# One matmul per level for both token tiles of a recurrence, its keys mixed by ScalarE

## The chip, the cores and the metric

The kernel runs on one core of a Trainium2 chip. A core has five engines that run side by side, each through its own list of instructions in order: TensorE (PE in the profile; PEld is its weight load), VectorE (DVE), ScalarE (ACT), GpSimd (POOL) and SyncE (SP), which issues most DMAs. The metric is the device time of one execution in microseconds. Three runs of the kernel before took 2759.31, 2762.63 and 2767.03 us (median 2762.63). Less is better.

## The reference

One layer over 2048 tokens of width 1024, in float32: a mixer, then a feed-forward block with a causal convolution. The mixer has two groups of four heads each, differential attention and a gated recurrence (HGRN2):

```python
proj = h @ w_in[l]                      # dq, dk, dv | hq, hf, hi, hg
# attention: a query sees all keys whose chunk of 64 tokens is not later than its own
mask = k_chunk[None, :] <= q_chunk[:, None]
a = softmax(q0 k0) - lam * softmax(q1 k1);  o = a @ v
# recurrence, chunks of 64 tokens: f = lb + (1 - lb) * sigmoid(f_logit), k = 1 - f
b = cumsum(log f)                       # within the chunk
att[t, s] = sum_k q[t, k] k[s, k] exp(b[t, k] - b[s, k])   for s <= t
o = att @ v + (q * exp(b)) @ state
state = exp(b_last) * state + (k * exp(b_last - b))^T @ v
x = x + concat([o_diff, o_hgrn]) @ w_out;   x = x + ConvGLU(RMSNorm(x))
```

The order of tokens inside a pair of 64-token chunks is free as long as the causal order of the recurrence and the mask of the attention follow it: attention sums over keys, and each output row goes back to its own token.

## The kernel before

The mixer stage goes over four sections `s`, one per head pair (one attention head, one recurrence head), and inside a section over eight blocks of 256 tokens, `BLK`; a block is two token tiles of 128 (`g` or `j` is 0 or 1). For each block it runs projections (`proj_a`, `proj_b`, `proj_c`, matmuls in fp32r with tiles `WA`, `WB`, `WC`), transposes, attention (`attn`, `attn_o`) and the recurrence (`hgrn`, `hgrn_o`). Sections and blocks are interleaved: the projections of block b+1 run beside the attention and the recurrence of block b. The step order is a string (`ORDER`, `O0`, `OF`), and on top of it the instructions of a block are merged by the program's scheduler, so that the matmuls of several steps alternate on TensorE.

The recurrence works without divisions. `hgrn` builds the decay products by doubling: `LEVELS` are half widths h of 1, 2, 4, ... 64. At level h a token tile of 128 is cut into groups of 2h; queries of the later half of each group meet keys of the earlier half. Three tiles are updated in place: `qP` holds queries times decay, `kS` keys times decay, `TT` the products of whole groups. One level does this:

- two matmuls (L441), one per token tile: the stationary operand is `kS` of the tile (127 to 64 columns), the moving operand the 64 queries of the later halves; the result is `lt[:, g]`, in PSUM. These are plain float32, and the profile shows each as two records.
- two predicated copies on DVE (L444), one per token tile: what the byte mask `lmask` marks is put into the attention tile `att[g]` of 128 x 128.
- three products on DVE (L449, L450, L452): the queries of the later halves times the first half's product, the keys of the earlier halves times the second half's, and the new `TT`.

The next level's matmuls read the new `qP` and `kS`; `lt` has one PSUM buffer (`HB=1`, shared with `op` and `sp` of `hgrn_o`), so they also wait for both copies. `hgrn_o` then multiplies `att` with the values and updates the state. The attention tiles rotate over three buffers. The scores `sc` of the attention also have one buffer: matmuls fill it, DVE takes the maximum (L367), ACT the exponential (L378), and only then may the next scores be written.

`load_rest` makes the masks once, on POOL, during the first block. The stage after the mixer, `load_o`, reads the mixer's output back, transposes it on TensorE and splits it by ACT and DVE (L555, L556) for the output projection. The later stages (up projection, down projection) are not touched.

Of the kernel before, what the change touches and what calls it, by code (L numbers as in the profile page):

```python
# [25 lines left out]
TOP, FEW, SMALL, SMALL2 = 480, 192, 320, 192  # L26
# [34 lines left out]

@with_exitstack
def hymba_kernel(ctx, tc, x, ln1_w, w_in, q_norm_w, k_norm_w, lam_q1, lam_k1, lam_q2, lam_k2,
                 diff_subln_w, hgrn_lb_logits, hgrn_norm_w, w_out, ln2_w, w_up, conv_w, conv_b,
                 w_down, out):
# [52 lines left out]
    lmask = few.tile([P, 7, 64], U8, name="lmask")  # L118
    NATT = 3
    atts = [cst.tile([P, P], F32, name=f"att{n}") for n in range(NATT)]  # L120
# [14 lines left out]
    def load_rest(tmp, tmq):  # L135
        lamv = tmp[:, 0:256].rearrange("p (n e) -> p n e", n=4)
        lbd = tmp[:, 256:268].rearrange("p (n e) -> p n e", n=3)
        lmf = tmq[:, 0:448].rearrange("p (l e) -> p l e", l=7)
# [27 lines left out]
        for li, h in enumerate(LEVELS):  # L166
            v = lmf[:, li, :].rearrange("p (n h) -> p n h", h=h)
            n = 64 // h
            for pat, base, mul in (([-2 * h, n], 0, 1), ([2 * h, n], h - 1, -1)):
                POOL.affine_select(out=v, in_=v, pattern=[pat, [0, h]], compare_op=ALU.is_ge,  # L170
                                   fill=0.0, base=base, channel_multiplier=mul)
        POOL.tensor_copy(out=lmask, in_=lmf)
        for a in atts:
            POOL.memset(a, 0.0)
# [10 lines left out]
    with ExitStack() as ms:  # L185
        wp = pool(ms, "wp", 1)
        kv = pool(ms, "kv", KVB, side="right")
# [25 lines left out]
        def phase1(b):  # L213
# [3 lines left out]
            for j in range(2):  # L217
                xt = pb.tile([P, D], F32, name="xt", tag="p")
                dma(out=xt, in_=x[b * BLK + j * P:b * BLK + (j + 1) * P, :])
                xts.append(xt)  # L220
# [35 lines left out]
        for s in range(4):  # L256
# [87 lines left out]
            def attn(b, j):  # L344
# [9 lines left out]
                for si, (k0, k1) in enumerate(segs):  # L354
                    for c in range(2):
# [8 lines left out]
                        if last:  # L364
                            DVE.memset(sc[0:64, w - 64:w], -3.0e38)
# [61 lines left out]
            def hgrn(b):  # L427
# [481 lines left out]
```

## Time and profile before

| | us |
|---|---|
| median of three runs | 2762.63 |
| the profiled execution | 2761.66 |
| its span in the trace | 2760.0 |
| TensorE busy (share of the span) | 2662.2 (96%) |
| VectorE busy | 1892.9 (69%) |
| ScalarE busy | 1212.4 (44%) |
| GpSimd busy | 1053.6 (38%) |

The mixer stage lasts from the start to about 1230 us of the span; the output projection follows until about 1600, the up projection until about 2100, the down projection to the end. Busy time is the union of an engine's records, and the end of a matmul's record is modelled: consecutive matmuls overlap in the trace. What a matmul takes on a full TensorE is therefore read from start to start.

### The profile page before, as it was taken

To read this page: it belongs to the slowest core of one execution; us is meant where nothing else is said; L and a number is where in the kernel's file an instruction comes from. 1 tells how busy PE (TensorE), PEld (TensorE's weight loads), DVE (VectorE), ACT (ScalarE), POOL (GpSimd) and SP (SyncE) were. 2 spreads that over 40 slices of the span, in tenths; PEclk is the share of its full clock that TensorE was granted. 3 is DMA by queue.
4 is the path that set the end of the run, shared out by engine and by line. 5 is a ranking of instruction groups with operands and counts; after the bars stand their busy time and mean duration, and the time that the engine had idled before them with its cause. 6 is when DMAs were issued, how large, how long until landed. Compare 5 with 4: busy or idle time off the path is not lost. (4 is left out here: it accounts for less than half of the span.)

```text
span 2760.0 us, 43193 instructions
## 1 busy us (share of the span) xinstructions
PE 2662.2 (96%) x15170; PEld 2329.6 (84%) x15170; DVE 1892.9 (69%) x4051; ACT 1212.4 (44%) x2878; POOL 1053.6 (38%) x1153
## 2 busy tenths in 40 slices
PE   7999999999999999989999999999999998899999
PEld 6888999999999999978877888887888886687887
DVE  4667855676667666773338666668777768978787
ACT  4555544454345444454335344345434434334332
POOL 2222222212222222220334443444344347877775
PEclk9999999999999999999999999999999999999999
DMA  5333422232222322125754232225222234775754
GB/s 183 119 109 112 130 89 86 82 124 83 99 83 75 115 91 84 50 88 172 248 192 142 83 92 75 86 92 175 77 85 91 70 92 129 170 159 132 178 172 168
DMA packets 273494, 322.96 MB, mean 117 GB/s; under 512 B 19470, under 2 KB 238974, under 8 KB 269182
## 3 DMA queue, kind: packets, MB, share of 16 engines
q1 hardware_dynamic: 266366, 295.04, 32.8%
q0 software_dynamic: 6912, 25.17, 5.3%
q8 instruction: 120, 1.97, 0.3%
q14 instruction: 96, 0.79, 0.1%
HBM read 198.50 MB, written 104.86 MB: 110 GB/s over the span
## 5 line engine op out<-in xcount | busy, mean ns | idle before, releaser
L684 PE MATMUL q<-xT,WS 128*128 128x512 f32 x704 | 274.4, 390 | 2.4 <-DVE xT L617 2.4
L683 PE MATMUL q<-xT,WS 128*128 128x512 f32 x704 | 274.4, 390 | 0.5 <-ACT xT L616 0.5
L685 PE MATMUL q<-xT,WS 128*128 128x512 f32 x704 | 274.3, 390 | 0.6 <-DVE WS L617 0.4
L797 PE MATMUL pd<-TW,SG 128*128 128x512 f32 x616 | 245.1, 399 | 21.2 <-DVE acc L803 7.1
L799 PE MATMUL pd<-TW,SG 128*128 128x512 f32 x616 | 243.2, 396 | 2.2 <-DVE SG L617 2.2
L798 PE MATMUL pd<-TW,SG 128*128 128x512 f32 x616 | 244.0, 397 | 0.5 <-DVE TW L617 0.5
L616 ACT CAST WS<-st 128x512 fp32r<-128x512 f32 x176 | 108.4, 618 | 243.6 <-PE q L685 227.1
L684 PE MATMUL q<-xB,WS 128*128 128x512 f32 x528 | 205.9, 390 | 2.2 <-DVE xB L617 2.2
L685 PE MATMUL q<-xB,WS 128*128 128x512 f32 x528 | 206.1, 390 | 1.2 <-DVE WS L617 1.2
L683 PE MATMUL q<-xB,WS 128*128 128x512 f32 x528 | 205.8, 390 | 0.7 <-ACT xB L616 0.7
L378 ACT ACTIVATE p<-sc,nm 128x1024 f32<-128x1024 f32 (+4 forms) x192 | 165.7, 863 | 90.3 <-DVE nm L367 87.5
L617 POOL TENSOR_TENSOR WS<-st,WS 128x512 fp32r<-128x512 f32 x44 | 88.2, 2004 | 278.4 <-ACT WS L616 258.8
L252 PE MATMUL pj<-WA,hT 128*128 128x384 f32 x512 | 176.4, 344 | 4.1 <-DVE hT L239 4.1
L367 DVE TENSOR_REDUCE nm<-sc 128x1 f32<-128x1024 f32 (+4 forms) x192 | 174.5, 909 | 6.9 <-PE sc L363 4.3
L253 PE MATMUL pj<-WA,hT 128*128 128x384 f32 x512 | 175.3, 342 | 0.0
L254 PE MATMUL pj<-WA,hT 128*128 128x384 f32 x512 | 174.5, 341 | 0.0
L797 PEld LDWEIGHTS pd<-TW,SG 128*128 128x128 f32 x616 | 118.1, 192 | 52.1 <-DVE acc L803 7.6
L684 PEld LDWEIGHTS q<-xT,WS 128*128 128x128 f32 x704 | 132.3, 188 | 30.4 <-DVE xT L617 3.1
L685 PEld LDWEIGHTS q<-xT,WS 128*128 128x128 f32 x704 | 132.3, 188 | 29.0 <-DVE WS L617 1.4
L683 PEld LDWEIGHTS q<-xT,WS 128*128 128x128 f32 x704 | 132.4, 188 | 28.6 <-ACT xT L616 0.9
L616 ACT CAST WS<-rawu 128x512 fp32r<-128x512 f32 x132 | 82.0, 623 | 159.2 <-PE q L685 159.2
L252 PE MATMUL pjc<-hT,WC 128*128 128x256 f32 x512 | 151.6, 296 | 0.2 <-ACT ig L321 0.2
(412 smaller groups left out, 7857.3 us busy)
## 6 DMA issues: line engine op xcount, KB each, us to landing
hT<-hTd SPq DMA_DIRECT2D x24, 2048.0 KB, 7.9
rawu<-in_w_up_dram SPq DMA_DIRECT2D x176, 256.0 KB, 3.1
x2d<-acc POOLq DMA_DIRECT2D x48, 512.0 KB, 6.5
gd<-c SPq DMA_DIRECT2D x176, 128.0 KB, 1.8
G<-gd SPq DMA_DIRECT2D x24, 768.0 KB, 4.2
xt<-in_x_dram SPq DMA_DIRECT2D x32, 512.0 KB, 4.1
hTd<-hT SPq DMA_DIRECT2D x8, 2048.0 KB, 6.2
qT<-qh SPq DMA_DIRECT2D x256, 64.0 KB, 2.0
```

What stands on the lines that cost most here:

```text
L252: PE.matmul(dst, lhsT=lh, rhs=rh, start=dt == 0, stop=False)
L253: PE.matmul(dst, lhsT=lh, rhs=rl, start=False, stop=False)
L254: PE.matmul(dst, lhsT=ll, rhs=rh, start=False, stop=dt == ND - 1)
L367: DVE.tensor_reduce(out=nm, in_=sc[:, 0:w], axis=AX.X, op=ALU.max, negate=True)
L378: ACT.activation(out=p[:, 0:w], in_=sc[:, 0:w], func=AF.Exp, bias=nm, accum_out=l)
L616: ACT.copy(dst[:, 0], src)
L683: PE.matmul(dst, lhsT=w[:, 0, cs], rhs=b_[:, 0, dt], start=dt == 0, stop=False)
L684: PE.matmul(dst, lhsT=w[:, 0, cs], rhs=b_[:, 1, dt], start=False, stop=False)
L685: PE.matmul(dst, lhsT=w[:, 1, cs], rhs=b_[:, 0, dt], start=False, stop=dt == 3)
L797: PE.matmul(pd, lhsT=Sx[n][:, 0, k], rhs=w[:, 0], start=k == 0, stop=False)
L798: PE.matmul(pd, lhsT=Sx[n][:, 0, k], rhs=w[:, 1], start=False, stop=False)
L799: PE.matmul(pd, lhsT=Sx[n][:, 1, k], rhs=w[:, 0], start=False, stop=k == len(qs) - 1)
```

## The change

1. In the mixer the second token tile of each block now runs backwards: the host hands over a second copy of `x`, `xm`, whose odd tiles of 128 rows are reversed, and `phase1` reads that one. The mask of the attention follows (`attn`), and `load_o` turns the odd tiles round again while it reads the transposed tile from PSUM (`tv[:, :, ::-1]`).
2. With the mirrored tile the earlier halves of tile 0 and the earlier halves of tile 1 stand in complementary columns. At each level ACT copies these 64 + 64 keys into a new tile `kp` of 128 columns (two buffers), and one matmul with 128 stationary and 128 moving columns replaces the two of 64. Its result has both tiles' products in `lt`, and the predicated copies, now over all 128 partitions, take what their mask marks. In the last block of the last section DVE makes the copy.
3. The masks are two sets (28 selects on POOL, 14 before), the attention tiles four (two per token tile), and both lie in a pool of their own at the top of the memory during the mixer. A padding is 64 bytes smaller.

```diff
-TOP, FEW, SMALL, SMALL2 = 480, 192, 320, 192
+TOP, FEW, SMALL, SMALL2 = 480, 128, 320, 192
+def view(a, off, *dims):
+
+    return bass.AP(a.tensor, a.offset + off, [list(a.ap[0])] + [list(d) for d in dims if d[1] > 1])
...
-                dma(out=xt, in_=x[b * BLK + j * P:b * BLK + (j + 1) * P, :])
+                dma(out=xt, in_=xm[2 * b + j])
...
                         if last:
-                            DVE.memset(sc[0:64, w - 64:w], -3.0e38)
+                            if j:
+                                DVE.memset(sc[64:P, w - P:w - 64], -3.0e38)
+                            else:
+                                DVE.memset(sc[0:64, w - 64:w], -3.0e38)
...
-        POOL.tensor_copy(out=lmask, in_=lmf)
-        for a in atts:
+        POOL.tensor_copy(out=lmask[:, :, 0:7], in_=lmf)
+        for a in atts[0] + atts[1]:
             POOL.memset(a, 0.0)
...
+        mc = pool(ms, "mc", 1, side="right")
+        lmask = mc.tile([P, 2, 8, 64], U8, name="lmask")
+        atts = [[mc.tile([P, P], F32, name=f"att{g}{n}") for n in range(2)] for g in range(2)]
...
-                att = [atts[(2 * b + g) % NATT] for g in range(2)]
+                att = [atts[g][b % 2] for g in range(2)]
                 for li, h in enumerate(LEVELS):
-                    nb = BLK // (2 * h)
-                    nk = P - h
+                    n, m = 64 // h, P // h
+                    qv = view(qP, h, (P - h, 2), (2 * h, n), (1, h))
+                    kl = view(kS, 0, (2 * h, n), (P + h, 2), (1, h))
+                    kf = view(kS, 0, (P + h, 2), (2 * h, n), (1, h))
                     lt = ps.tile([P, 2, 64], F32, name="lt", tag=HT, bufs=HB)
-                    qv = qP.rearrange("p (n two h) -> p n two h", two=2, h=h)
-                    kvw = kS.rearrange("p (n two h) -> p n two h", two=2, h=h)
-                    for g in range(2):
-                        ng = nb // 2
-                        PE.matmul(lt[0:nk, g].rearrange("p (n h) -> p n h", h=h), lhsT=kS[:, g * P:g * P + nk],
-                                  rhs=qv[:, g * ng:(g + 1) * ng, 1, :], start=True, stop=True)
+                    kp = wk.tile([P, P], F32, name="kp", tag="kp", bufs=2)
+                    kd = view(kp, 0, (2 * h, n), (h, 2), (1, h))
+                    if s == 3 and b == NB - 1:
+                        DVE.tensor_copy(out=kd, in_=kl)
+                    else:
+                        ACT.copy(kd, kl)
+                    PE.matmul(view(lt, 0, (64, 2), (h, n), (1, h)), lhsT=kp, rhs=qv, start=True, stop=True)
                     for g in range(2):
                         DVE.copy_predicated(
-                            out=att[g][0:nk].rearrange("p (n two h) -> p n two h", two=2, h=h)[:, :, 1, :],
-                            mask=lmask[0:nk, li].rearrange("p (n h) -> p n h", h=h),
-                            data=lt[0:nk, g].rearrange("p (n h) -> p n h", h=h))
+                            out=att[g].rearrange("p (n two h) -> p n two h", two=2, h=h)[:, :, 1 - g, :],
+                            mask=lmask[:, g, li].rearrange("p (n h) -> p n h", h=h),
+                            data=lt[:, g].rearrange("p (n h) -> p n h", h=h))
...
-                cs = slice(hf * 512, hf * 512 + 512)
-                ACT.copy(oT[0][:, cs], tp)
-                DVE.tensor_tensor(out=oT[1][:, cs], in0=tp, in1=oT[0][:, cs].bitcast(F32), op=ALU.subtract)
+                tv, (oh, ol) = tp.rearrange("p (q c) -> p q c", c=P), [
+                    t[:, hf * 512:hf * 512 + 512].rearrange("p (q c) -> p q c", c=P) for t in oT]
+                if i % 2:
+                    tv = tv[:, :, ::-1]
+                ACT.copy(oh, tv)
+                DVE.tensor_tensor(out=ol, in0=tv, in1=oh.bitcast(F32), op=ALU.subtract)
```

The three products of a level stay three instructions of the same size, written with `qv`, `kf` and `T` by the new views. The loop that makes the masks runs over both `g`.

How this stands on the engines is shown at the turn from section 1 to section 2 (the recurrence of the last block of a section beside the first projections of the next one). TensorE, from the first level to the second, before:

```order
L441 MATMUL lt<-qP,kS 127x64 x2
L252 MATMUL pj<-WA,hT 128x384
L253 MATMUL pj<-WA,hT 128x384
L254 MATMUL pj<-WA,hT 128x384
L252 MATMUL pj<-WA,hT 128x384
L362 MATMUL sc<-kst,qT 128x512
L363 MATMUL sc<-kst,qT 128x512
L362 MATMUL sc<-kst,qT 128x384
L363 MATMUL sc<-kst,qT 128x384
L441 MATMUL lt<-qP,kS 126x64 x2
```

And with the change:

```order
L454 MATMUL lt<-qP,kp 128x128
L259 MATMUL pj<-WA,hT 128x384
L260 MATMUL pj<-WA,hT 128x384
L258 MATMUL pj<-WA,hT 128x384
L259 MATMUL pj<-WA,hT 128x384
L368 MATMUL sc<-kst,qT 128x512
L369 MATMUL sc<-kst,qT 128x512
L368 MATMUL sc<-kst,qT 128x384
L369 MATMUL sc<-kst,qT 128x384
L454 MATMUL lt<-qP,kp 128x128
```

The same eight matmuls stand between two levels; the two level matmuls have become one.

VectorE at the fifth level of the same block, before (the copies, the product of the queries, that of the keys, with attention's small operations between):

```order
L444 COPY_PREDICATED att_92<-lmask,lt 112x4x16
L444 COPY_PREDICATED att_90<-lmask,lt 112x4x16
L449 TENSOR_TENSOR qP<-qP,TT 128x8x16
L382 SCALAR_TENSOR_TENSOR l_8370<-l,wv 128x1
L450 TENSOR_TENSOR kS<-kS,TT 128x8x16
```

With the change:

```order
L456 COPY_PREDICATED att_186<-lmask,lt 128x4x16
L456 COPY_PREDICATED att_188<-lmask,lt 128x4x16
L460 TENSOR_TENSOR qP<-qP,TT 128x2x4x16
L391 SCALAR_TENSOR_TENSOR l_8494<-l,wv 128x1
L461 TENSOR_TENSOR kS<-kS,TT 128x2x64
```

The product of the keys now stands two levels ahead of that of the queries: its tile has the shape of the seventh level beside the fifth level's copies.

ScalarE around the first levels of the same block, before (`p,l<-sc` is the exponential of the scores, `qr`, `vst` and `qn` belong to the next block's projections):

```order
L485 ACTIVATE op,ssh<-o_8304 128x128
L378 ACTIVATE p,l<-sc,nm 128x1024
L283 COPY qr<-pj 128x256
L284 COPY vst<-pj 128x128
L286 ACTIVATE qn<-qr 128x256
L372 ACTIVATE wv<-nm,nm_8346 128x1
L378 ACTIVATE p,l<-sc,nm_8346 128x896
L283 COPY qr<-pj 128x256
```

With the change:

```order
L496 ACTIVATE op,ssh<-o_8428 128x128
L387 ACTIVATE p,l<-sc,nm 128x1024
L453 COPY kp<-kS 128x128
L289 COPY qr<-pj 128x256
L290 COPY vst<-pj 128x128
L292 ACTIVATE qn<-qr 128x256
L453 COPY kp<-kS 128x128
L381 ACTIVATE wv<-nm,nm_8470 128x1
L387 ACTIVATE p,l<-sc,nm_8470 128x896
L453 COPY kp<-kS 128x128 x2
L289 COPY qr<-pj 128x256
```

Nothing has changed places; the copies into `kp` are put in between. Those of levels one and two stand further up, before the last exponentials of the block before.

## Rows read from the trace of the kernel before

**Rows 1.** Stretches of the mixer: length, busy PE PEld DVE ACT POOL, PE clock

```profile
60.00:300.00 240.00, 227.87 (x1672) 214.24 (x1670) 170.00 (x550) 131.01 (x376) 64.14 (x126) 1.00 0.33 113
300.00:620.00 320.00, 313.71 (x2316) 296.41 (x2316) 217.18 (x731) 153.20 (x449) 70.33 (x135) 1.00 0.31 99
620.00:920.00 300.00, 294.58 (x2164) 279.48 (x2165) 202.36 (x686) 140.55 (x418) 69.29 (x133) 1.00 0.29 95
920.00:1230.00 310.00, 296.15 (x2143) 277.86 (x2142) 207.62 (x686) 141.78 (x414) 73.62 (x129) 0.98 0.24 79
```

**Rows 2.** The tile lt: what TensorE waited for before its matmuls (us, times)

```profile
  DVE kS L450: 13.3, 18
```

**Rows 3.** Timeline of TensorE, first level of one block: start, duration (us), instruction

```profile
621.26 0.34 PE L254 MATMUL pj<-WA,hT 128*128 128x384 f32 x1
621.43 0.56 PE L441 MATMUL lt<-qP,kS 128*127 128x64 f32 x4
621.80 0.42 PE L252 MATMUL pj<-WA,hT 128*128 128x384 f32 x1
622.05 0.34 PE L253 MATMUL pj<-WA,hT 128*128 128x384 f32 x1
```

**Rows 4.** Timeline of TensorE, seventh and last level of the same block

```profile
635.59 0.28 PE L254 MATMUL pj<-WB,hT 128*128 128x256 f32 x1
635.71 0.28 PE L252 MATMUL pj<-WB,hT 128*128 128x256 f32 x1
635.92 0.45 PE L441 MATMUL lt<-qP,kS 128*64 128x64 f32 x4
636.30 0.38 PE L253 MATMUL pj<-WB,hT 128*128 128x256 f32 x1
636.52 0.28 PE L254 MATMUL pj<-WB,hT 128*128 128x256 f32 x1
```

**Rows 5.** Timeline of TensorE, a lone float32 matmul of 128 by 128

```profile
868.11 0.33 PE L253 MATMUL pj<-WA,hT 128*128 128x384 f32 x1
868.28 0.39 PE L477 MATMUL sp<-ig,kt__11715 128*128 128x128 f32 x2
868.42 0.42 PE L254 MATMUL pj<-WA,hT 128*128 128x384 f32 x1
868.68 0.34 PE L252 MATMUL pj<-WA,hT 128*128 128x384 f32 x1
868.86 0.33 PE L253 MATMUL pj<-WA,hT 128*128 128x384 f32 x1
```

**Rows 6.** ScalarE on a 128x128 tile, memory to memory: min/median/max ns

```profile
L323 ACT ACTIVATE sg<-ig x64: 296/310/334, 35.5 to 1179.1; 128x128 f32<-128x128 f32 x64
```

**Rows 7.** Predicated copies, two levels, 60 to 1230 us: busy us, mean ns

```profile
L444 DVE COPY_PREDICATED att<-lmask,lt 126x64 f32<-126x64 uint8 x62 | 15.7, 304 | 3.3 <-PE lt L441 2.1
L444 DVE COPY_PREDICATED att<-lmask,lt 120x64 f32<-120x64 uint8 x64 | 12.2, 222 | 4.3 <-PE lt L441 4.3
```

**Rows 8.** Timeline of VectorE, fifth level of the block of Rows 3

```profile
630.97 0.36 DVE L444 COPY_PREDICATED att<-lmask,lt 112x64 f32<-112x64 uint8 x2 [0.38 <-PE lt L441]
631.24 0.28 DVE L449 TENSOR_TENSOR qP<-qP,TT 128x128 f32<-128x128 f32 x1
631.57 0.29 DVE L450 TENSOR_TENSOR kS<-kS,TT 128x128 f32<-128x128 f32 x1
```

**Rows 9.** The tile sc: what its engines waited for (us, times)

```profile
  ACT p L378: 21.8, 54
```

**Rows 10.** Timeline of GpSimd, the masks

```profile
18.58 6.03 POOL L170 TENSOR_SCALAR_AFFINE_SELECT tmq<-tmq 128x64 f32<-128x64 f32 x14
...
28.42 0.19 POOL L98 TENSOR_SCALAR rq_m<-ssq 128x4 f32<-128x4 f32 x1 [3.19 <-DVE ssq L288]
```

**Rows 11.** Groups by line, 1200 to 1600 us: the split in load_o

```profile
L556 DVE TENSOR_TENSOR oT<-tpo,oT 128x512 fp32r<-128x512 f32 x32 | 21.8, 686 | 7.4 <-ACT oT L555 7.4
L555 ACT CAST oT<-tpo 128x512 fp32r<-128x512 f32 x32 | 18.3, 582 | 52.9 <-PE tpo L553 52.9
```

More of the change, by code (lines that the diff above doesn't have):

```diff
@@ L64, in hymba_kernel @@
                  diff_subln_w, hgrn_lb_logits, hgrn_norm_w, w_out, ln2_w, w_up, conv_w, conv_b,
-                 w_down, out):
+                 w_down, xm, out):
     nc = tc.nc
@@ L117, in hymba_kernel @@
     hgw = cst.tile([P, P], F32, name="hgw")
-    lmask = few.tile([P, 7, 64], U8, name="lmask")
-    NATT = 3
-    atts = [cst.tile([P, P], F32, name=f"att{n}") for n in range(NATT)]
     def load_ln1(tp):
@@ L137, in load_rest @@
         lbd = tmp[:, 256:268].rearrange("p (n e) -> p n e", n=3)
-        lmf = tmq[:, 0:448].rearrange("p (l e) -> p l e", l=7)
+        lmf = tmq[:, 0:896].rearrange("p (g l e) -> p g l e", g=2, l=7)
         for hf in range(2):
@@ L165, in load_rest @@
         POOL.memset(lmf, 1.0)
[L166 to L171, printed above, removed]
-        POOL.tensor_copy(out=lmask, in_=lmf)
-        for a in atts:
+        for g in range(2):
+            for li, h in enumerate(LEVELS):
+                v = lmf[:, g, li, :].rearrange("p (n h) -> p n h", h=h)
+                n = 64 // h
+                for pat, base, mul in (([-2 * h, n], -g * h, 1), ([2 * h, n], h - 1 + g * h, -1)):
+                    POOL.affine_select(out=v, in_=v, pattern=[pat, [0, h]], compare_op=ALU.is_ge,
+                                       fill=0.0, base=base, channel_multiplier=mul)
+        POOL.tensor_copy(out=lmask[:, :, 0:7], in_=lmf)
+        for a in atts[0] + atts[1]:
             POOL.memset(a, 0.0)
@@ L446, in hgrn @@
-                            mask=lmask[0:nk, li].rearrange("p (n h) -> p n h", h=h),
-                            data=lt[0:nk, g].rearrange("p (n h) -> p n h", h=h))
-                    Tv = T.rearrange("p (n two) -> p n two", two=2)
-                    DVE.tensor_tensor(out=qv[:, :, 1, :], in0=qv[:, :, 1, :], in1=Tv[:, :, 0:1].broadcast_to([P, nb, h]), op=ALU.mult)
-                    DVE.tensor_tensor(out=kvw[:, :, 0, :], in0=kvw[:, :, 0, :], in1=Tv[:, :, 1:2].broadcast_to([P, nb, h]), op=ALU.mult)
@@ L451, in hgrn @@
-                    Tn = TT[:, to:to + nb]
-                    DVE.tensor_tensor(out=Tn, in0=Tv[:, :, 0], in1=Tv[:, :, 1], op=ALU.mult)
+                            out=att[g].rearrange("p (n two h) -> p n two h", two=2, h=h)[:, :, 1 - g, :],
+                            mask=lmask[:, g, li].rearrange("p (n h) -> p n h", h=h),
+                            data=lt[:, g].rearrange("p (n h) -> p n h", h=h))
+                    DVE.tensor_tensor(out=qv, in0=qv, in1=view(T, 0, (m + 1, 2), (2, n), (0, h)), op=ALU.mult)
@@ L453, in hgrn @@
+                    DVE.tensor_tensor(out=kf, in0=kf, in1=view(T, 1, (m - 1, 2), (2, n), (0, h)), op=ALU.mult)
+                    Tn = TT[:, to:to + m]
+                    DVE.tensor_tensor(out=Tn, in0=view(T, 0, (2, m)), in1=view(T, 1, (2, m)), op=ALU.mult)
                     T = Tn
-                    to += nb
+                    to += m
                 HG[b] = (qk, kS, qP, T)
@@ L458, in hgrn_o @@
                 qk, kS, qP, T = HG.pop(b)
-                att = [atts[(2 * b + g) % NATT] for g in range(2)]
+                att = [atts[g][b % 2] for g in range(2)]
                 for g in range(2):
@@ L903 @@
         args.append(nc.dram_tensor(f"in_{name}_dram", a.shape, mybir.dt.from_np(a.dtype), kind="ExternalInput").ap())
+    xm = np.array(inputs["x"]).reshape(S // P, P, D)
+    xm[1::2] = xm[1::2, ::-1]
+    arrays["in_xm_dram"] = xm
+    args.append(nc.dram_tensor("in_xm_dram", xm.shape, F32, kind="ExternalInput").ap())
     args.append(nc.dram_tensor("out_0_dram", (1, S, D), F32, kind="ExternalOutput").ap())
```

## The prediction, before the result was known

> **What bounds the kernel now.** I read the engines' busy time by stretches first, then the waits at the tile that the change touches, then the timeline of TensorE at that place. In the mixer, where all of the edit but one detail lies, TensorE is busy 227.87 + 313.71 + 294.58 + 296.15 = 1132.3 of 1170 us between 60 and 1230 us, at a granted clock of 0.98 to 1.00, its level of 2.4 GHz; VectorE is busy some two thirds of that time and ScalarE under half (153.20 of 320 us in the second stretch) [rows 1]. The reader is to see there that only 38 us are free on TensorE. So this stage ends when TensorE has worked off its list, and what counts is how long each group of matmuls holds it, and what it newly waits for. The recurrence looks like a chain (matmul, copies, products, next matmul), but its links are hidden between other matmuls: TensorE stood before the level matmuls 18 times, 13.3 us in all, over 224 levels [rows 2].
>
> **The change part by part.** *Level matmuls.* There are 4 sections x 8 blocks x 7 levels = 224 levels. What a group costs is read from start to start. At the first level the matmul before it starts at 621.26 and the second one behind it at 622.05: 0.79 us, in which two 384-column matmuls stand that take 0.175 each in an undisturbed stream (868.68 to 868.86 is 0.18); so the four records of the group cost 0.79 - 0.35 = 0.44 us [rows 3, 5]. At the seventh level it is 636.52 - 635.71 = 0.81, less two of 256 columns at 0.12: 0.57 [rows 4]. Seven groups of this block read this way; the first and last are shown, and the five between give 0.44, 0.44, 0.42, 0.40 and 0.36. The mean is 3.07 / 7 = 0.439 us, so the level matmuls hold TensorE for 224 x 0.439 = 98 us.
>
> With the change a level is one float32 matmul of 128 by 128, two records. That shape is in the trace: between two 384-column matmuls it costs 868.68 - 868.11 - 0.35 = 0.22 us [rows 5]. I take this value. The step from its own start to the next one is 0.14, so it can't cost less than that (saving 67 us), and from above it is bounded by the 0.44 of the four records (saving nothing). The saving is 224 x (0.439 - 0.22) = 49 us, and nothing lies beside it: the engine is full, and the same matmuls stand between two levels as before, in the same order.
>
> The row shows that a group's time goes with its count of records, about 0.11 us each, and little with the columns that move (64 or 128) [rows 3, 5]. The Trainium skill (TensorE: Matmul & The Clock Gate, Back-to-back issue gap) gives for an isolated stream about 60 cycles up to 64 columns and 134 at 128: four short ones then cost 240 cycles and two long ones 268, the change would save nothing, and the sum would stand at some 2764 us by that estimate. The same page (LDWEIGHTS) has a weight load at its columns / 1.2 ns, 107 ns for 128: two loads fewer would save 213 ns a level, 48 us, also an estimate. The trace agrees with the second.
>
> *The copies into kp.* 217 on ScalarE and 7 on VectorE (the last block). The nearest row, a 128 x 128 operation of ScalarE from memory to memory, takes 310 ns [rows 6]: 217 x 0.31 = 67 us. It is spread over the mixer, some 17 us on a section of about 300 us where ScalarE works 153 of 320 [rows 1]; it becomes 55% busy. The first two levels' copies pick single keys or pairs in turn from two tiles. A fine pattern has a price on VectorE here: the predicated copy takes 304 ns at the second level and 222 at the fourth [rows 7]. With the same 0.08 us on 62 of the copies ScalarE has 5 us more, which its idle time hides as well.
>
> What may come onto the path is the copy's place: the level matmul now waits for ScalarE. What takes the edge off is that the product of the keys no longer waits for a level matmul, only for the copy; it is issued two levels ahead. From the copies' start at 630.97 the queries' product is done at 631.52 and the keys' at 631.86 [rows 8]; the later one leaves the path between two levels, 0.34 us, and a matmul with half the records gives its result sooner. Behind a copy that waits on ScalarE stand the next block's `qr`, `vst`, `qn` and the exponentials of the scores, and TensorE waits for those, the exponential before all, as `sc` has one buffer: 21.8 us in 54 waits now, weight loads included [rows 9].
>
> The trace doesn't show the new wait, so I bound it: from below the present 13.3 us at the level matmuls could vanish (-13 us) [rows 2]; from above every copy stands in the chain with its full 0.31 us (+67 us) [rows 6]. Between ends so far apart I take the value nearest to a row: half of the 13.3 us once more, +7 us, because ScalarE's free time and the lead of two levels speak for little.
>
> *VectorE.* Two predicated copies and three products a level as before, of the same count of elements; 7 copies more. Nothing. If four-dimensional patterns cost 0.08 us as above on six operations of a level or so, VectorE would have some 224 x 0.4 = 90 us more and at 75% to 80% would still not bound.
>
> *Masks.* 14 more selects, 6 us, stand on GpSimd ahead of `rq_m`, which waited 3.19 us for its input before; it slips by some 3 us [rows 10]. The projections that TensorE has in hand then cover it; without that cover it would cost those 3 us once.
>
> *The reversed read in `load_o`.* 16 of the 32 operations of each engine, 582 and 686 ns [rows 11]. If each took twice as long, 16 x (0.58 + 0.69) = 20 us on engines that are not full in that stage; I cost it at nothing. `xm` is read as `x` was. The tiles' new places cost nothing that a row could show.
>
> **Sum.** Against the profiled execution of 2761.7 us (the median of the runs is 1 us more): 2761.7 - 49 + 7 = 2720 us, 1.5% faster.
>
> **The rivals.** *The saving comes back in part as waits at the new link.* For it: ScalarE's list is worked off in order, and some copies stand right behind an exponential of about 1 us or ahead of two levels' matmuls. Against it: the order puts them early. If half the copies' time shows, 33 us in place of 7: 2761.7 - 49 + 33 = 2746 us.
>
> *Time goes with the columns that move.* Then nothing is saved and the copies hide: 2762 us and up to 7 more. (The first of the two rules of the Trainium skill above, TensorE: Matmul & The Clock Gate, would have it so.) Against it stand the four records at 0.44 us beside the two at 0.22 [rows 3, 5]; for it only that the lone matmul shown is followed by fp32r work, so that part of its load could be covered. No change.
>
> *ScalarE's list blocks the attention (the other side).* A copy waits for TensorE's level matmul two levels back, since `kp` has two buffers; the exponential of the scores stands behind it, and the next scores on TensorE wait for that. There are 192 exponentials; if each comes 0.35 us later (a copy with its wait) and the one score buffer passes all of it on, that is 67 us: 2761.7 - 49 + 67 = 2780 us. It decides from 49 / 192 = 0.26 us for each exponential. For it: 54 such waits exist already [rows 9]. Against: ScalarE is free half of the time, so a delay of one is made up before the next.
>
> **How the numbers follow.** My forecast (2700 to 2735) has 0.68, the partial return (2735 to 2753) 0.16, the columns or an almost full return 0.08, the blocked attention 0.08. What a measurement can tell from no change is 0.3%, about 8 us: below 2754 is faster. So faster 0.84, same 0.08, slower 0.08. The range goes from the saving with the present waits gone (2761.7 - 49 - 13 = 2700) up into the partial return, 2750.
>
> **What would show it.** Right: two records per level, 448 in all, their group at 0.22 to 0.28 us between fp32r matmuls; the mixer shorter by 40 to 50 us and the later stages as long as before; ScalarE 60 to 75 us busier; waits of TensorE at the level matmuls below 25 us. Wrong: the level group at 0.4 us (the price of the matmul failed), idle time of TensorE in the mixer well above 38 us with ScalarE named as releaser of `lt` or `sc` (the place of the copy failed), or the stage after the mixer longer by several us (the reversed reads).

## The result, and the profile after

The changed kernel takes 2786.5 us (median; 2783.2 to 2787.0) against 2762.6 for the kernel before beside it: a ratio of 1.0083 with a 95% interval of 1.0071 to 1.0096. It is slower by 0.8%, where 1.5% faster was forecast. Its profiled execution took 2783.2 us, with a span of 2781.4; before it was 2761.7 and 2760.0, so 21.4 us are to be found.

First the stretches of the mixer, with the columns of [rows 1] (busy PE, PEld, DVE, ACT, POOL, then the clock):

```profile
60.00:300.00 240.00, 222.68 (x1559) 208.28 (x1558) 162.79 (x538) 137.37 (x411) 61.62 (x123) 0.98 0.30 108
300.00:620.00 320.00, 308.21 (x2213) 288.46 (x2212) 222.12 (x738) 170.56 (x513) 69.63 (x137) 1.00 0.31 101
620.00:920.00 300.00, 292.39 (x2072) 273.85 (x2072) 205.94 (x697) 155.94 (x483) 69.48 (x135) 1.00 0.30 96
920.00:1230.00 310.00, 289.91 (x2025) 268.69 (x2024) 211.04 (x692) 155.91 (x471) 73.15 (x130) 0.97 0.23 72
```

TensorE is still busy 1113 of 1170 us, with fewer instructions. ScalarE has 17 us more in the second stretch, as forecast for one of this length, and 53 us more in the four together, where 60 to 75 were named. So the mixer has not become idle, and it has not become much shorter either. Where the time went is read from the first and last starts of three tiles: `pjc`, the mixer's last projection; `ot`, the load of the first output rows for the output projection; `q` from `xT`, the up projection (it starts at 1450 us, and not at about 1600, as the section on the time before has it). The numbers are x count, ns (min/median/max), first and last start. Before the change:

```profile
L254 PE MATMUL pjc<-hT,WC x512: 274/283/386, 39.3 to 1192.3; 128*128 128x256 f32 x171
L545 SPq DMA_DIRECT2D ot<-od x16: 319/382/431, 1189.7 to 1406.6; - x16
L683 PE MATMUL q<-xT,WS x704: 387/389/628, 1450.4 to 2293.3; 128*128 128x512 f32 x176
```

After it:

```profile
L260 PE MATMUL pjc<-hT,WC x512: 277/283/365, 39.8 to 1186.2; 128*128 128x256 f32 x171
L556 SPq DMA_DIRECT2D ot<-od x16: 320/376/423, 1248.1 to 1425.8; - x16
L697 PE MATMUL q<-xT,WS x704: 387/389/793, 1468.9 to 2315.2; 128*128 128x512 f32 x176
```

The mixer's last projection ends 6.1 us earlier (1192.3 to 1186.2). From there to the up projection it took 258.1 us, now 282.7: 24.6 us more. The rest of the program takes 2.9 us more (1309.6, 1312.5). -6.1 + 24.6 + 2.9 = 21.4. So there are two questions: why the handover from the mixer to the output projection lost 24.6 us, and why the mixer won 6 and not 42.

The handover first. `ot` was loaded at 1189.7, when the last block's recurrence had not yet begun, and its projection (`pjo`) filled TensorE between the last levels. Before the change:

```profile
1217.11 0.93 PE L441 MATMUL lt<-qP,kS 128*124 128x64 f32 x4
1217.80 0.77 PE L599 MATMUL pjo<-wo,oT 128*128 128x512 f32 x1
...
1220.69 0.39 PE L599 MATMUL pjo<-wo,oT 128*128 128x512 f32 x1
1220.92 0.53 PE L441 MATMUL lt<-qP,kS 128*120 128x64 f32 x4
```

Now `ot` is loaded at 1248.1. The timeline of the changed kernel there (start, duration, instruction, idle time before it and what ended it):

```profile
1208.56 0.77 PE L454 MATMUL lt<-qP,kp 128*128 128x128 f32 x2 [3.72 <-DVE kp L451]
...
1213.70 0.77 PE L454 MATMUL lt<-qP,kp 128*128 128x128 f32 x2 [1.94 <-DVE kp L451]
...
1247.73 0.32 SPq L434 DMA_DIRECT2D od<-oo  x1
1248.10 0.42 SPq L556 DMA_DIRECT2D ot<-od  x1
...
1251.78 1.97 PE L564 MATMUL tpo<-ident,ot 128*128 128x128 f32 x8 [6.12 <-DMA ot<-od]
...
1254.89 0.63 PE L614 MATMUL pjo<-wo,oT 128*128 128x512 f32 x1
1255.32 0.63 PE L615 MATMUL pjo<-wo,oT 128*128 128x512 f32 x1
```

In SyncE's list the load now stands right behind the mixer's last write (1247.73, 1248.10). TensorE has only some score matmuls to put between the last levels and waits there for a copy three times (3.72, 1.94 and 1.77 us). The first projection matmuls follow each other at 0.43 us (1254.89 to 1255.32), against 0.23 at 1340 us. The clock granted from 1250 to 1256 us is 0.50, the level of 1.2 GHz, after a wait of 6.12 us for the load. By thirds of a stretch of 90 us, before:

```profile
1190.00:1220.00 30.00, 20.69 (x125) 17.83 (x124) 24.19 (x51) 16.95 (x36) 12.34 (x10) 0.83 0.57 184
1220.00:1250.00 30.00, 28.34 (x188) 24.62 (x187) 20.87 (x51) 13.32 (x33) 3.43 (x8) 1.00 0.09 29
1250.00:1280.00 30.00, 29.76 (x155) 24.92 (x154) 8.55 (x16) 10.81 (x29) 2.73 (x7) 1.00 0.48 158
```

and after:

```profile
1190.00:1220.00 30.00, 15.99 (x67) 11.92 (x67) 27.94 (x67) 14.67 (x29) 10.48 (x10) 0.72 0.38 112
1220.00:1250.00 30.00, 20.12 (x125) 17.67 (x123) 12.29 (x34) 10.31 (x28) 4.87 (x8) 0.79 0.06 16
1250.00:1280.00 30.00, 27.32 (x119) 22.33 (x120) 5.50 (x8) 5.46 (x14) 0.74 (x2) 0.86 0.39 134
```

468 matmuls became 311 (14 of the difference are records saved at the levels), and the granted clock fell from 1.00 to 0.79 in the middle third.

Why the load went there is not in the trace; it follows from the memory map of the two programs (bytes per partition). The change puts 3,072 bytes at the top and two copies of `kp`, 1,024 bytes, into the working pool, so all pools of that side lie 4,096 bytes lower; the pools of the other side lie 2,048 lower. The output projection's last tile, `ht`, lay at 132,096 to 136,192 before, over the mixer's projection pool, which is done early. Now it lies at 130,048 to 134,144 and covers 704 bytes of `sm` (133,440 to 136,164), the small statistics, which are in use until the mixer's last output. If the scheduler therefore holds the projection's first steps back until the statistics are free, a shift of the pools alone must bring the loss and take it away; that is tested below.

### The profile page after: what moved, and what is told of

It reads as the page before. It is cut to its first block, busy times and chain, and to the rows that moved or that the text cites. A ratio compares the mean times of both kernels' runs of the same rounds, so it can differ in the third digit from the quotient of the medians.

```text
span 2781.4 us, 42701 instructions
## 1 busy us (share of the span) xinstructions
PE 2650.1 (95%) x14722; PEld 2305.0 (83%) x14722; DVE 1900.0 (68%) x4058; ACT 1263.6 (45%) x3095; POOL 1051.6 (38%) x1168
## 5 line engine op out<-in xcount | busy, mean ns | idle before, releaser
L425 PE MATMUL av<-vst,aT 128*128 128x128 f32 x1088 | 153.0, 283 | 7.6 <-ACT aT L422 7.2
```

## The experiments

All times are medians; a ratio is to the kernel before, run on the same chip (2762.4 to 2763.7 us). Two theories stood first. "Places": the tiles' new places cost the handover, whatever the recurrence does. "ScalarE in the key path": the copies of the mixed keys block the attention and the last block. Each predicts a slower kernel, by about as much.

### The places

The recurrence of before at the new places:

```diff
-TOP, FEW, SMALL, SMALL2 = 480, 192, 320, 192
+TOP, FEW, SMALL, SMALL2 = 480, 128, 320, 192
...
-    lmask = few.tile([P, 7, 64], U8, name="lmask")
...
-    atts = [cst.tile([P, P], F32, name=f"att{n}") for n in range(NATT)]
...
+        mc = pool(ms, "mc", 1, side="right")
+        mcs = mc.tile([P, 2, 8, 64], U8, name="lmask")
+        lmask = mcs[:, 0, 0:7]
+        atts = [mc.tile([P, P], F32, name=f"att{n}") for n in range(NATT)]
+        mc.tile([P, P], F32, name="attpad")
...
+        wk.tile([P, 2 * P], F32, name="kpad", tag="kpad", bufs=1)
```

> The recurrence of the kernel before, untouched, with the change's places alone: mask and attention tiles at the top, 1,024 bytes more in the working pool, so that the output projection's pools lie where they lie in the changed kernel. Theory 'places': the projection's first load of the outputs again stands behind all of the mixer's writes, the stretch from the last block's diagonal to the up stage grows by some 20 to 26 us (248 to 270-274), and the whole comes to 2780-2789 us. Theory 'ScalarE in the key path': nothing of the recurrence has changed, so 2762 us within 0.3%.

Measured 2786.5 us, ratio 1.0087 (1.0073 to 1.0101): the whole loss, with not one instruction of the recurrence changed.

```profile
L258 PE MATMUL pjc<-hT,WC x512: 274/283/386, 38.5 to 1191.3; 128*128 128x256 f32 x171
L549 SPq DMA_DIRECT2D ot<-od x16: 319/380/424, 1255.1 to 1432.0; - x16
L687 PE MATMUL q<-xT,WS x704: 388/389/628, 1476.1 to 2317.7; 128*128 128x512 f32 x176
```

The mixer ends as before (1191.3), `ot` comes at 1255.1, and the handover takes 284.8 us. The reverse, the changed recurrence with the old places:

```diff
+    lmask = few.tile([P, 2, 8, 64], U8, name="lmask")
+    atts = [[cst.tile([P, P], F32, name=f"att{g}{n}") for n in range(1)] for g in range(2)]
...
-        mc = pool(ms, "mc", 1, side="right")
-        lmask = mc.tile([P, 2, 8, 64], U8, name="lmask")
-        atts = [[mc.tile([P, P], F32, name=f"att{g}{n}") for n in range(2)] for g in range(2)]
...
-                att = [atts[g][b % 2] for g in range(2)]
+                att = [atts[g][0] for g in range(2)]
```

> The changed recurrence with mask and attention tiles back at their old place (one attention tile per token tile instead of two, so that they fit). Theory 'places': the handover is as before the change (248 us from the last block's diagonal to the up stage), what the mixer gained stays, 2752-2760 us. Theory 'ScalarE in the key path': the loss stays, 2780-2787 us.

Measured 2756.1 us, ratio 0.9978 (0.9968 to 0.9987).

```profile
L259 PE MATMUL pjc<-hT,WC x512: 274/283/365, 39.5 to 1181.6; 128*128 128x256 f32 x171
L555 SPq DMA_DIRECT2D ot<-od x16: 319/379/431, 1179.2 to 1397.4; - x16
L696 PE MATMUL q<-xT,WS x704: 388/389/796, 1440.5 to 2286.1; 128*128 128x512 f32 x176
```

The handover takes 258.9 us again. Third, the changed kernel with its tiles at the top but one attention tile per token tile (`for n in range(1)` in place of `range(2)`), so that the pools rise by 1,024 bytes and `ht` ends where `sm` does not yet begin (134,144 and 134,464):

> The changed kernel with one attention tile per token tile instead of two, still at the top; this alone moves the pools on that side up by 1,024 bytes, and the projection's last tile no longer lies over the statistics of the mixer. Theory 'places': as good as with the old places, 2752-2760 us, the same within 0.2%. Theory 'ScalarE in the key path': 2780-2787 us. A third, that it matters which bank or end of the memory the masks lie at, would set it apart from the kernel with the old places.

Measured 2757.8 us, ratio 0.9981 (0.9973 to 0.9990). With that the top of the memory is cleared: 1,024 bytes decide on 29 us, and "places" holds. "ScalarE in the key path" falls as the cause of the loss. That it is the overlap of `ht` and `sm`, and no other of the shifted tiles, follows from the map; no run moved `ht` alone.

### What the merge is worth

That leaves the mixer. Without the mixed tile, at the old places (`lhsT=kp` becomes `lhsT=kS[:, 0:P]`, and the copies go; it leaves tile 1's keys out):

> As the changed recurrence at the old places, but without the mixed tile: the shared matmul reads tile 0's keys for both token tiles, which leaves tile 1's keys out of the diagonal. It prices the mixing. Theory 'ScalarE in the key path': without 224 copies and the wait at each level the mixer gives back what the merge promised, 30 us or more less than with the copies, 2715-2730 us. Theory 'the mixer is bound by more than the level's records': less than 12 us, 2742-2755 us.

Measured 2750.5 us, ratio 0.9950 (0.9937 to 0.9964): the copies cost 5.6 us, and without them the merge still brings only 12. The kernel before with the merge alone:

```diff
-                    for g in range(2):
-                        ng = nb // 2
-                        PE.matmul(lt[0:nk, g]..., lhsT=kS[:, g * P:g * P + nk], rhs=qv[:, g * ng:(g + 1) * ng, 1, :], ...)
+                    PE.matmul(lt[0:nk]..., lhsT=kS[:, 0:nk],
+                              rhs=qv[:, :, 1, :].rearrange("p (g n) h -> p g n h", g=2), start=True, stop=True)
```

> The kernel before, with nothing but the two level matmuls of a block made into one: both token tiles' queries meet tile 0's keys, so tile 1's keys are left out; masks, attention tiles, their places and the vector steps are those of before. The forecast's price (0.439 us for the four records, 0.22 for two, 224 levels) gives 2762 - 49 = 2713 us. The price of the least disturbed groups in their places (0.278 for four, 0.138 for two) gives 2762 - 31 = 2731 us. Theory 'waits take back most of it', drawn from the run without the copy: 2748-2752 us.

Measured 2753.7 us, ratio 0.9969 (0.9957 to 0.9981): 8.7 us for 448 records less. In the other direction, the records of six levels taken away (`if li == 0` ahead of the matmuls), and every level's pair issued twice:

> The kernel before with the matmul of the first level alone; the predicated copies of the other six read its result again, so the six levels' products are left out, and 192 of 224 four-record groups with them. By the forecast's price (0.439) 84 us less, 2678 us; by the least disturbed price (0.278) 53 us less, 2709 us; if the mixer is paced by its chain of vector steps and waits and not by TensorE's records, less than 30 us, 2732-2755 us.

> The kernel before with every level's two matmuls issued twice, the same values written again: 896 more records. By the forecast's price (0.439 a group) 98 us more, 2861 us; by the least disturbed price (0.278) 62 us more, 2825 us; if the waits around a group can hold further records, less than 40 us, 2775-2800 us.

Measured 2724.1 us (0.9860, 0.9846 to 0.9874) and 2844.6 us (1.0297, 1.0282 to 1.0311). 768 records less give 38 us, 0.05 each; 896 more cost 82, 0.09 each; 448 less by the merge give 0.02 each. The second time falls between the two prices named for a record, 0.09 being most of the forecast's. The first falls short of both and misses the theory that the mixer is paced by something else as well (2732 to 2755). So added work costs more than removed work gives back. Part of this may be the clock: with one level it is granted at 0.96 from 60 to 300 us, at 1.00 before. By the starts of `f` from `pjc`, the first eight blocks win 7 us and the twenty behind them 32, which is 0.07 us a record in these.

With the copies on VectorE (`DVE.tensor_copy(out=kd, in_=kl)` for all 224, old places):

> The changed recurrence at the old places with all 224 copies of mixed keys on VectorE instead of ScalarE. Rival 'the copy's place in ScalarE's list costs the 6 us that the kernel without a copy saves': no wait for another engine stands before a level any more, 2748-2753 us. Rival 'VectorE's list is the recurrence's own chain': 217 copies of some 0.22 us lengthen it by 48 us, of which a part comes out, 2760-2775 us.

Measured 2760.7 us, ratio 0.9993 (0.9984 to 1.0002), 4.6 us more than with ScalarE, as the rival "VectorE's list" had it (2760 to 2775): the change's choice of engine is the better one.

### Turns between TensorE and VectorE

A theory of what takes the saving back: a level's matmul, the copies, the products and the next matmul take turns. From the run with the merge alone, TensorE and VectorE at the sixth and seventh level of a block:

```profile
677.99 0.28 DVE L448 TENSOR_TENSOR kS<-kS,TT 128x128 f32<-128x128 f32 x1
678.00 0.28 PE L254 MATMUL pjc<-hT,WC 128*128 128x256 f32 x1
678.12 0.28 PE L252 MATMUL pjc<-hT,WC 128*128 128x256 f32 x1
...
678.42 0.43 PE L439 MATMUL lt<-qP,kS 128*96 128x128 f32 x2
...
678.89 0.35 DVE L442 COPY_PREDICATED att<-lmask,lt 96x64 f32<-96x64 uint8 x2 [0.35 <-PE lt L439]
```

The projection matmul at 678.12 is worth 0.12 us; the level could start at 678.24, and starts at 678.42, behind the key product that ends at 678.27. These 0.18 us stand in no list of idle time, since the ends of records overlap; they are seen from start to start alone. If the turn were shorter, the wait would go. So the products were put ahead of the copies, and four levels' results side by side into one bank, so that the next matmul need not wait for the copies:

```diff
+                    if li % 4 == 0:
+                        lt4 = ps.tile([P, 4, 2, 64], F32, name="lt", tag=HT, bufs=HB)
+                    lt = lt4[:, li % 4]
...
+                    DVE.tensor_tensor(out=qv, ...)   # both products moved ahead of the copies
+                    DVE.tensor_tensor(out=kf, ...)
                     for g in range(2):
                         DVE.copy_predicated(...)
```

> The changed kernel with one attention tile per token tile (2757.8 us), and in each level the query and key products ahead of the two predicated copies in VectorE's list; four levels' results lie side by side in one PSUM bank, so that the next level need not wait for the copies. Theory 'lock-step' (a level's matmul, the vector steps and the next level's matmul take turns, and TensorE's saving is lost in waiting for them): the turn gets shorter by some 0.4 us and a good part of the waits at the levels goes, 2725-2748 us. Rival 'the waits at the levels are not what holds the mixer': the same as without the swap within 4 us, 2754-2762 us.

> The same swap and the same bank in the kernel before (2762.5 us), whose level keeps its two matmuls. Theory 'lock-step': there the waits at the levels are some 17 us of 20 blocks, and about half of it goes: 2740-2755 us, a smaller gain than in the merged kernel. Rival: 2758-2766 us.

> The same swap and the same bank in the kernel before with the merged matmul alone (2753.7 us; tile 1's keys are left out of the diagonal). Theory 'lock-step': the merge pays what its records are worth once the turn is short, 2715-2738 us, and the difference to the swapped kernel with two matmuls is 15-31 us instead of 8.7. Rival: 2750-2758 us, difference 8-10 us.

> The kernel before with four levels' results side by side in one bank, and the vector steps in their old order. The copies still stand ahead of the products in VectorE's list, so by 'lock-step' the turn is as long as before: 2758-2766 us. If it is the one result buffer that holds the levels, 2740-2755 us, as with the swap.

Measured 2759.2 (0.9988, 0.9980 to 0.9997), 2767.7 (1.0021, 1.0012 to 1.0029), 2756.0 (0.9980, 0.9971 to 0.9989) and 2762.1 (0.9998, 0.9989 to 1.0007). No run gained, and the second lost 5 us, so the order inside a level does not hold the mixer. "Lock-step" as it was put has fallen. In the third run the same waits at the levels are there (0.43 us for a lone group, 0.12 of it before its start, read as in the table below): the other work in VectorE's list, such as the row maxima of about 1 us, stands between the products.

So VectorE's list itself was the next suspect; from a block's first level to its last it is busy 84% before and 86% with the merge (19 blocks, from the timelines). Two runs leave the predicated copies out, one moves the products of totals (`POOL.tensor_tensor(out=Tn, ...)`):

> The merged matmul in the kernel before (tile 0's keys alone) without the 448 predicated copies: the levels' results are not taken over, so the diagonal is left out. It takes 14 x 0.23 = 3.2 us of VectorE's work out of each block's levels, a stretch of 12.6 us that VectorE fills to 86%. Theory 'VectorE's list bounds the stretch with the levels': with the list slack the merge pays 20 to 31 us against the same kernel with two matmuls (next run), some 2715-2730 us. Rival 'what the merge saves is lost elsewhere': the difference stays at 9 us, 2740-2752 us.

> The kernel before, two matmuls a level, without the 448 predicated copies (the diagonal is left out). By 'VectorE's list' TensorE bounds this one, so little is won by taking vector work away: 2742-2756 us. If VectorE alone bounded the stretch already before, as much is won as with the merge, 2715-2730 us.

> The changed recurrence at the old places (2756.1 us) with the 224 products of the groups' totals on GpSimd, which is busy for a quarter of the mixer, instead of VectorE: 7 x 0.18 = 1.3 us less in VectorE's list for each block's levels. Theory 'VectorE's list': 5 to 20 us faster, 2736-2751 us. Rival: 2754-2760 us, or slower, if the products (0.45 us there by GpSimd's row of 128x128) come too late for the next level.

Measured 2757.5 (0.9977, 0.9968 to 0.9986), 2786.4 (1.0089, 1.0074 to 1.0105) and 2762.1 (0.9998, 0.9989 to 1.0006). Both times miss what was named for them. The difference between the first two is 29 us, as the theory wanted, but for the wrong reason: the kernel with two matmuls became 24 us *slower* by doing less. VectorE's share is not the explanation, and its work moved to GpSimd cost 6 us.

### The order between two levels

What had changed with every edit is the order. The scheduler makes it anew, and seems to put the next level where it takes the previous one to be done. Counted in TensorE's list (projection and score matmuls at their pitch, the rest at 0.1 us a matmul), the work between two levels of a block is 1.61 us before, 1.59 with the merge alone, 1.42 with the change, 1.23 without the predicated copies. The last runs hold a level back by edges that only order TensorE's list:

```diff
+AFTER = {
+    "0.0.1": "I-798", "0.0.5": "I-984", ...    # section.block.level: behind which matmul
+            def after(mm, key):
+                if key in AFTER:
+                    tc.add_manual_dep(mm.ins, AFTER[key], mybir.DependencyInfo(
+                        mybir.DependencyClass.NoSync, mybir.DependencyReason.DATA), reason="fill")
...
-                    PE.matmul(view(lt, 0, (64, 2), (h, n), (1, h)), lhsT=kp, rhs=qv, start=True, stop=True)
+                    mm = PE.matmul(view(lt, 0, (64, 2), (h, n), (1, h)), lhsT=kp, rhs=qv, start=True, stop=True)
+                    after(mm, f"{s}.{b}.{li}")
```

> The changed recurrence at the old places (2756.1 us), with 121 order-only edges that hold a level's matmul in TensorE's list until matmuls worth 1.4 us stand between it and the level before (mean between two levels 1.81 us; without the edges 1.42, in the kernel before 1.61). No work is added or left out. Theory 'fill': TensorE waits at the levels because the order, which was made from the shorter levels, puts too little work between them for VectorE's steps; the waits in and around the level groups go from 33 us to about half, 2736-2750 us. Rival 'no order helps, the waits only move': 2753-2762 us.

> The same with 159 edges and at least 1.8 us between two levels (mean 2.27 us). Theory 'fill': the waits at the levels are nearly gone, but the recurrence of a block ends later: 2730-2755 us. If the recurrence's end holds the block, slower than with 1.4 us, 2760-2790 us. Rival: 2753-2762 us.

> The kernel before without the 448 predicated copies (2786.4 us, slower by 24 us for less work; the diagonal is left out), with 130 edges that put at least 1.4 us of matmuls between two levels (mean 1.71 us; without the edges 1.23). Theory 'fill': the loss came from the order, and goes: 2745-2764 us. Rival: it stays, 2780-2790 us.

Measured 2743.2 (0.9929, 0.9917 to 0.9941), 2757.7 (0.9980, 0.9971 to 0.9989) and 2788.6 us (1.0090, 1.0077 to 1.0104). The first is as the theory "fill" had it, the other two as its rivals had it. The first is also the best complete kernel of the study, 0.7% faster than before and 12.8 us faster than the same instructions in the scheduler's own order. One level of it:

```profile
668.94 0.28 PE L259 MATMUL pjc<-hT,WC 128*128 128x256 f32 x1
669.05 0.39 PE L458 MATMUL lt<-qP,kp 128*128 128x128 f32 x2
669.20 0.36 PE L257 MATMUL pjc<-hT,WC 128*128 128x256 f32 x1
669.40 0.28 PE L258 MATMUL pjc<-hT,WC 128*128 128x256 f32 x1
```

It starts at once (669.05 behind 668.94 plus 0.12) and costs 669.40 - 668.94 - 0.24 = 0.22 us. Taken from start to start in the same way, for every whole group that stands alone among projection and score matmuls, 355 to 1053 us (mean; of it the delay before its start):

| kernel | groups | mean us | delay |
|---|---|---|---|
| before | 81 | 0.465 | 0.037 |
| merge alone | 93 | 0.431 | 0.123 |
| without a copy | 96 | 0.390 | 0.110 |
| change, old places | 68 | 0.316 | 0.053 |
| with 1.4 us between levels | 98 | 0.288 | 0.044 |

So the order of the same instructions is worth 12.8 us in the changed kernel; that is shown. That the amount of work between two levels is what counts is not shown. At 1.8 us the first eight blocks take 324 us and not 310 (by the start of each block's second `sg`), while the twenty behind them take 698 with either. The merge alone has as much work there as the kernel before (1.59 and 1.61) and three times the delay. The kernel without predicated copies did not get its 24 us back, although 1.71 us lie between its levels. Read as in the table, a lone group costs it 0.58 us, 0.13 of it before its start, and with the edges 0.53 and 0.09: the price came down, the time did not. The cause of these 24 us is open.

## Why the prediction was wrong

**What bounds the kernel: right as a reading, too much as a conclusion.** TensorE fills the mixer, before and after. But "this stage ends when TensorE has worked off its list" treats its list as given. Part of what the profile shows as busy is short waits between overlapping records (0.12 us at a lone group with the merge alone), and the list is made anew with every edit.

**The price of the records: right for an undisturbed group, too low in place.** There are 448 of them (the first line of the fence on the waits below), and an undisturbed group costs what was forecast:

```profile
624.93 0.34 PE L369 MATMUL sc<-kst,qT 128*128 128x384 f32 x1
625.11 0.39 PE L454 MATMUL lt<-qP,kp 128*128 128x128 f32 x2
625.25 0.43 PE L260 MATMUL pj<-WA,hT 128*128 128x384 f32 x1
625.51 0.34 PE L258 MATMUL pj<-WA,hT 128*128 128x384 f32 x1
```

625.51 - 624.93 - 0.35 = 0.23 us, against 0.44 for four records [rows 3]. The rival that time goes with the columns has fallen. The Trainium skill's rule of weight loads (TensorE: Matmul & The Clock Gate, LDWEIGHTS) agrees with the 0.21 us between these two rows, and its price for isolated short matmuls (Back-to-back issue gap), by which both groups would cost nearly the same, does not.

But 0.22 us was taken for all 224 levels, and the mean of the lone groups is 0.32 at the old places and 0.29 in the best kernel. Against 0.465 before, that is 33 and 40 us (224 levels) in place of 49.

**The saving of 49 us, "nothing lies beside it: the engine is full, and the same matmuls stand between two levels as before, in the same order": a step that failed.** The order was read at one place and did not stay: 1.61 us between two levels became 1.42. The mixer's last projection came 6.1 us earlier in the trace, 10.7 at the old places, and 20.1 (at 1172.2 us) with the edges; so 29 of the 49 are missing even there. Where they are can be read from TensorE's own records, each counted from its start to the next one's, from 60 us to the mixer's last projection (us):

| kernel | level matmuls | projections | scores | transposes `tpa` | the rest | sum |
|---|---|---|---|---|---|---|
| before | 73.9 | 660.5 | 141.2 | 53.3 | 203.4 | 1132.3 |
| change, old places | 44.1 | 664.4 | 145.6 | 62.2 | 205.1 | 1121.4 |
| with 1.4 us between levels | 37.6 | 668.5 | 146.1 | 60.4 | 199.5 | 1112.1 |

The level matmuls give 30 and 36 us and not 49. Other matmuls take 19 and 16 us of it back, the transposes of the attention weights (`tpa`) 9 and 7. Of these some 5 lie where the next block's `tpq` comes straight behind a `tpa`: 7 times for 2.0 us before, 21 times for 7.8 at the old places, 20 times for 7.3 with the edges. That is again the order. The weight loads behind the transposes also wait longer for ScalarE's copy, 60 to 1230 us (us in all, times, longest). Before:

```profile
PEld av L416 <- ACT aT L413: 11.0, 37, 1.0
```

and in the best kernel:

```profile
PEld av L424 <- ACT aT L421: 15.0, 39, 2.4
```

Of these 4 us, 3 lie ahead of the mixer's last projection. So it is known where the time went. Why the projections and the scores take more is not; no run told it apart.

**"The tiles' new places cost nothing that a row could show": the step that turned the sign.** No row of before could show it, but the step was taken as harmless for that reason. The places cost 24 us by themselves, and 29 to 30 in the changed kernel. None of the rivals had it; the one that ended on the other side named the attention, which the old places refute at 2756 us. The sign that the prediction gave for its reversed reads, a longer stage after the mixer, did appear, but from the places.

**New waits at the level matmuls, +7: near the 5.6 us measured without a copy, but by luck.** The 13.3 us of [rows 2] add the wait of a weight load and that of its matmul for the same moment, and the longest of both is one wait in the last block (at 1214.6 us). Before, 60 to 1230 us:

```profile
PE lt L441 <- DVE kS L450: 5.0, 6, 3.5
...
PEld lt L441 <- DVE kS L450: 7.4, 10, 3.7
```

So half of 13.3 is no measure of a wait. The tile `lt` in the changed kernel: its matmuls, and what ended the idle time ahead of its instructions (us, times):

```profile
L454 PE MATMUL lt<-qP,kp x448: 270/275/583, 47.6 to 1221.6; 128*128 128x128 f32 x150
...
  DVE kp L451: 7.4, 3
  ACT kp L453: 5.5, 4
```

The 7.4 are the last block's, where the handover was lost. The 5.5 stand at the first two levels of the first block (47.6 and 50.4 us), again with load and matmul both counted; behind them no idle time at a level names ScalarE. The 5.6 us that the copies cost are thus not idle time that the lists show at `lt`. A copy takes 298 ns (median; 309 on the mean), 310 were assumed [rows 6].

**Reversed reads, masks, fine patterns: right.** The split in `load_o` takes 582 and 686 ns as in [rows 11]; the masks take 10.11 us, and `rq_m` starts 1.4 us later than in [rows 10] (29.83 for 28.42, where 3 were forecast); the predicated copies take 245 ns on the mean, as before. Two side sums are off and bear on nothing: ScalarE was to be 55% busy, where (153 + 17) / 320 is 53%, and six operations at 0.08 us are 0.48 a level and not 0.4.

```profile
L570 DVE TENSOR_TENSOR oT<-tpo,oT 128x512 fp32r<-128x512 f32 x32 | 21.8, 686 | 13.8 <-ACT oT L569 13.8
L569 ACT CAST oT<-tpo 128x512 fp32r<-128x512 f32 x32 | 18.4, 582 | 70.7 <-PE tpo L564 70.7
```

## What to carry to other kernels

Moving a tile moves its neighbours: compare the memory maps of both programs at the seams between stages, and look which late tile of the old stage lies under an early one of the new. Where a scheduler writes the order, an engine's saved time can be lost to the order that it makes anew: compare the whole list before and after, and not one place of it, since removing work can make a kernel slower, and try the same instructions in another order. Price an instruction by removing it and by doubling it: here a record was worth 0.02 to 0.05 us one way (the second with a lower clock in a part of the run) and 0.09 the other. Read waits for one engine at a time: the waits of a weight load and of its matmul are often the same wait.

## What the runs showed of the hardware

A stationary operand of 64 columns between matmuls of 128 costs the same with two records as with four. At the seventh level, with the merge alone and two records:

```profile
679.64 0.28 PE L252 MATMUL pjc<-hT,WC 128*128 128x256 f32 x1
679.85 0.43 PE L439 MATMUL lt<-qP,kS 128*64 128x128 f32 x2
680.21 0.39 PE L253 MATMUL pjc<-hT,WC 128*128 128x256 f32 x1
680.43 0.28 PE L254 MATMUL pjc<-hT,WC 128*128 128x256 f32 x1
```

680.43 - 679.64 - 0.24 = 0.55 us, as much as the four records of [rows 4] at 0.57, where two records of 96 to 127 columns cost down to 0.22. Of the 27 such groups of either kernel that stand alone, none costs less than 0.55, and 17 of the merged ones cost 0.55 or 0.56. With the mixed tile, whose 128 columns are always full, the seventh level costs 0.22 as well (the lower half of its groups in the best kernel). So part of what the change saves at that level, 0.35 us, comes from the shape and not from the count of records. The Trainium skill (TensorE: Matmul & The Clock Gate, LDWEIGHTS) has the load's time go with its columns. The trace agrees for the load's own record, some 0.13 us with 64 columns and 0.19 with 128, but the group with the shorter loads is the dearer one; why is not shown.
